# A hybrid decoder trunk on one core: the order of tasks in a step, two more chunks turned on VectorE, one unit more ahead of their high parts, and narrower score matmuls

## Chip, cores and metric

One core of one Trainium2 chip. The metric is the device time of one execution in microseconds (us). Engines are named PE (TensorE, matmuls), DVE (VectorE), ACT (ScalarE), POOL (GpSimd) and SP (which only issues DMAs here).

## What is computed

A decoder of two layers over x, 256 positions x 2048 columns, float32, with 256 memory tokens. Per layer:

```
h = rmsnorm(x); P = h @ W_in        four mixers on columns of P:
  A  forgetting attention, 4 heads x 128 ("fox")
  B  latent attention, low-rank q and kv with a rotary key, 4 heads ("mla")
  C  causal spatial gating unit, 4 groups x 128
  D  differential attention, 4 heads
x += concat(A, B, C, D) @ W_o
x += cross_attention(rmsnorm(x), rmsnorm(mem))      4 heads, W_cq, W_ck, W_cv, W_co
x += (silu(n @ W_gate) * (n @ W_up)) @ W_down, n = rmsnorm(x)     hidden width 5632
```

After the second layer the output is rmsnorm(x).

## The kernel before

**Products in three matmuls.** Each float32 factor is split into a high part (rounded to the fp32r type) and a low part (the rest). A product is hi*hi + hi*lo + lo*hi, each an fp32r matmul. For a weight, ACT casts the high part (`high`, L204) and DVE subtracts it for the low part (`low`, L210). A few units named in `POOLED` (L40) have their low part made on POOL instead.

**Units.** The weight matrices are walked in groups (one output block of 512 columns, or less, over all of its contraction). A group is cut into units of 1024 weight columns: at 512 output columns a unit has two contraction tiles k of 128 rows. `drive` (L227) makes one list of all units of both layers, in order. For each unit it issues the high and low parts of the unit three places ahead (`convert`, `AHEAD = 3`), then the unit's matmuls (at 512 columns: two k, two halves of the positions, three products, 12 matmuls), then the group's `done` if it was the last one, and then `self.step()`. With `hold=1`, used for the first chunk of w_co, the list reads: chunk 0's first unit, chunk 1's first unit, chunk 0's second, chunk 1's second, and then chunks 2 and 3. A chunk of w_co has two units, a chunk of w_o eight.

**Tasks.** Everything between the matmuls is written as Python generators that issue some instructions and then yield. `soon` puts one in the list `urgent`, `later` in the queue `background` (with one empty step ahead of it); only attention heads go there. `step` (L193) advances each urgent task to its next yield, then the first two of the background. A task may wait for others with `wait`, which yields until they are done. Each engine runs its instructions in the order in which they were issued; the kernel's own order is kept (`manual_schedule`). So a step's place in that order says behind what an instruction queues.

**Chunks of x.** x lives as four chunks of 512 columns. When an output block of w_o, w_co or w_down is complete, `into_x` (L945) adds it to its chunk (two DVE adds, L950) and starts a task `norm_chunk` (L342): ACT sums the squares, two yields follow, and then the chunk is turned (positions to the free dimension), and split into high and low parts with the norm's gains (`split_turned`: ACT L206, DVE L212) in two halves, with a yield behind each. There are two ways to turn. Without `early`, `turn` (L414) issues four PE transposes of 128x128 into PSUM for each half. With `early`, `turn_blocks` (L422) issues 16 DVE transposes of 32 partitions x 256 elements (32x32 blocks), four to a step. Before the change, `early` is set for chunks 0 to 2 of w_o in both layers and of the last w_down blocks in the first layer, and never for w_co.

**Who needs a chunk.** A group's operands are a `Split`. Ahead of its matmuls, a unit calls `need(k)` (L104), which drains the tasks of chunk k // 4: it runs them to their end there and then, so that whatever they had not issued comes in front of the unit's matmuls. Behind w_co comes gate: its first unit (k 0 and 1) needs chunk 0, its third chunk 1.

**Heads.** `attend` (L486) takes the MLA and fox heads through scores (L440), mask, exponent, `normalise` (L473, behind a DVE reciprocal L468), transposes and output (L500) over some seven steps. `attend_memory` (L1056) does the same for cross-attention; its first two heads wait for `tq` and `tk` and then take one more empty step (`if h < 2`). `out_v` (L1103) drains two heads and issues their output matmuls (L1116), which read a copy (L1079) of the transposed probabilities. `gate_norm` (L760) and `gate_mix` (L780) are urgent tasks of the gating unit. Fox scores add an fp32r product (rows and own sums of log-forget) to the fp32 product of q and k; the second half of the queries needs 256 keys and the first only 128, but the fp32r product was given 256 columns in both (L439).

Of the kernel before, what the change touches and what calls it, by code (L numbers as in the profile page):

```python
# [12 lines left out]
F32R = mybir.dt.float32r  # L13
# [6 lines left out]
P = 128  # L20
T = 2
S = T * P
# [39 lines left out]
class Task:  # L62
# [5 lines left out]
    def step(self):  # L68
        if not self.done:
            try:  # L70
                next(self.gen)
            except StopIteration:
                self.done = True
# [68 lines left out]
class Kernel:  # L142
# [48 lines left out]
            yield  # L191

    def step(self):  # L193
        for t in list(self.urgent):
            t.step()
        self.urgent = [t for t in self.urgent if not t.done]
        for t in list(self.background)[:2]:
            t.step()
        self.background = deque(t for t in self.background if not t.done)


    def high(self, src, hi, scale=None):
# [24 lines left out]
    def drive(self, groups):  # L227

        units, held = [], []
        for g in groups:  # L230
            i, own = 0, []
            for src, kper in g.blocks:
                b = Block(src, kper * g.ncols)
                step = 1 if not units and not own else 1024 // g.ncols if g.ncols in (256, 512) else 2
                for k0 in range(0, kper, step):
                    n = min(step, kper - k0)
                    own.append(Unit(g, b, k0, n, i))
                    i += n
            if g.hold:
                units, held = units + own[: g.hold], own[g.hold :]  # L240
            else:
                units, held = units + own[: len(held)] + held + own[len(held) :], []
# [99 lines left out]
    def norm_chunk(self, st, c, g, name, early):  # L342

        nc, xs, stats, xc = self.nc, st[0], st[1], self.x[c]
        part = xs.parts[c] = self.split_tile(name)
        for t in range(T):
            self.square_sum(xc[:, t, :], stats[:, t, c : c + 1])
        st[4] += 1
        yield
        yield  # L350
        if early:
            raw = self.slot("xT")
            yield from self.turn_blocks(xc[:], raw)
        for b in range(2):
            tv = raw[:, 2 * b : 2 * b + 2, :] if early else self.turn(xc, 2 * b, 2, "xT")
            self.split_turned(tv, part, 2 * b, self.gains[:, g, 4 * c + 2 * b : 4 * c + 2 * b + 2])
            yield
# [75 lines left out]
    def scores(self, pairs, name="s"):  # L433

        ps = self.bank(name)
        first = True
        for q, off, nk in ((1, 0, S), (0, S, P)):
            for n, (x, y) in enumerate(pairs):
                w = S if x.dtype == F32R else nk  # L439
                self.nc.tensor.matmul(ps[:, off : off + w], x[:, q * P : (q + 1) * P], y[:, :w], start=first, stop=(q == 0 and n == len(pairs) - 1))  # L440
                first = False
        return ps

# [637 lines left out]
    def cross(self, l, norm, st, memT, mres):  # L1081
        s = {}
        y, cT = Split(1), norm[0]

        def out_q(ps):
            nat = self.slot("cq", shape=(P, T, 512))
            self.out_natural(ps, 0, 512, nat, self.times(norm[2][0], 128.0 ** -0.5))
            s["q"] = self.slot("cqT")
            yield
            yield from self.turn_blocks(nat[:], s["q"])  # L1090

        def done_q(ps):
            norm[3].drain()
            s["tq"] = self.soon(out_q(ps))

        def done_k(ps):
            self.mem_rms.drain()
            kT = self.slot("ckT")
            s["tk"] = self.soon(self.out_turned(ps, kT, mres[1]))
            s["p"] = [self.slot("cpT", shape=(P, 2, 512)) for _ in range(2)]  # L1100
            s["heads"] = [self.later(self.attend_memory((s["tq"], s["tk"]), s["q"], kT, h, s["p"][h // 2][:, h % 2, :])) for h in range(4)]

        def out_v(ps, hh):  # L1103
            if hh == 0:
                s["v"] = self.slot("cv", shape=(P, T, 512))
                y.parts[0] = self.split_tile("yc")
            v = s["v"]
            self.out_natural(ps, 0, 256, v[:, :, 256 * hh : 256 * hh + 256], mres[0])
            yield
            for t in s["heads"][2 * hh : 2 * hh + 2]:  # L1110
                t.drain()
            o = self.bank("co")
            for i in range(2):
                h = 2 * hh + i
                for kt in range(2):
                    self.nc.tensor.matmul(o[:, i * S : (i + 1) * S], v[:, kt, h * P : (h + 1) * P], s["p"][hh][:, i, kt * S : (kt + 1) * S], start=(i == 0 and kt == 0), stop=(i == 1 and kt == 1))  # L1116
            ov = o[:].rearrange("p (i s) -> p i s", i=2)
            self.split(ov, y.parts[0][0][:, 2 * hh : 2 * hh + 2, :], y.parts[0][1][:, 2 * hh : 2 * hh + 2, :])

        def done_v(hh):  # L1120
            def f(ps):
                s["tv%d" % hh] = self.soon(out_v(ps, hh))
                if hh == 1:
                    y.tasks[0] = [s["tv0"]]
                    y.late = s["tv1"]
            return f

        yield Group("cq", self.blocks("w_cq", l), 512, cT, False, done_q)
        yield Group("ck", self.blocks("w_ck", l), 512, memT, True, done_k)
        for hh in range(2):  # L1130
            yield Group("cv", self.blocks("w_cv", l, hh, 8), 256, memT, False, done_v(hh))
        for c in range(NC):
            yield Group("wco", self.blocks("w_co", l, c), 512, y, False, self.into_x(c, st, 2 + 3 * l, "fT"), hold=0 if c else 1)


    def ffn(self, l, norm, st):
# [211 lines left out]
```

## Time and profile before

| | |
|---|---|
| median of 3 runs | 2347.46 us (2346.2 to 2347.61) |
| the profiled execution, its own time | 2347.7 us |
| its span in the trace | 2346.0 us, 28353 instructions |
| PE / DVE / ACT / POOL busy | 99% / 64% / 48% / 11% of the span |
| granted PE clock, mean of the span | 0.999 |
| DMA | 444 MB, 189 GB/s |

The span runs from the first to the last instruction on the core; 1.7 us lie outside of it. A busy share is an average over all stages. A matmul's recorded duration is longer than the distance to the next one, since they are pipelined; what one costs is read from the distance of starts. In a timeline a row begins with the start (us from the span's start) and the duration, then engine, line, operation, out<-in, shapes and count; brackets give idle time before it and what ended it.

### The profile page before, as it was taken

What the parts mean: (1) busy time and instruction counts of PE and PEld (TensorE: products, weight loads), DVE (VectorE), ACT (ScalarE), POOL (GpSimd) and SP (SyncE); (2) the same over time, 40 slices, a digit from 0 to 9 for tenths busy, and PEclk for the clock granted to TensorE, in tenths of its full rate; (3) what the DMA queues carried; (4) which work ended last, traced back from release to release, by engine and by line L of the source; (5) the groups of instructions that cost most, each with busy time, mean ns of one, the idle gap of its engine ahead of it and who ended that gap; (6) DMA issues with size and microseconds to landing.
All of it is one profiled execution on the core that took longest, in us unless ns stands there. A gap on an engine that the chain in (4) does not pass through costs nothing.

```text
span 2346.0 us, 28353 instructions
## 1 busy us (share of the span) xinstructions
PE 2324.7 (99%) x10992; PEld 1950.3 (83%) x10992; DVE 1508.6 (64%) x2175; ACT 1132.2 (48%) x1611; POOL 251.3 (11%) x182
## 2 busy tenths in 40 slices
PE   9999999999999999999999999999999999999998
PEld 8888878888888888888898888798888888888886
DVE  6856687655766446767766666866666664476564
ACT  7656555644443334444455555545444443434443
POOL 1222341100000000000012314411000000000000
PEclk9999999999999999999999999999999999999999
DMA  8654555455455555555545454554555555555643
GB/s 293 223 177 154 186 189 188 164 193 200 179 208 195 189 197 181 196 200 184 203 164 193 161 176 159 201 197 162 197 180 197 202 194 196 197 180 192 221 179 126
DMA packets 69719, 444.24 MB, mean 189 GB/s; under 512 B 8000, under 2 KB 10064, under 8 KB 19920
## 3 DMA queue, kind: packets, MB, share of 16 engines
q1 hardware_dynamic: 67328, 435.52, 52.4%
q0 software_dynamic: 2112, 6.85, 0.9%
q8 instruction: 86, 1.41, 0.2%
q14 instruction: 49, 0.40, 0.0%
q10 hardware_dynamic: 144, 0.06, 0.0%
HBM read 440.30 MB, written 2.10 MB: 189 GB/s over the span
## 4 chain that ended last, share of the span: by engine, by line
PE 88%; DVE 4%; ACT 2%; DMA 2%; issue 1%; POOL 1%; SPq 0%; POOLq 0%; ACTq 0%; DVEq 0%
PE gate L305 7%; PE gate L304 7%; PE gate L303 7%; PE up L305 7%; PE up L304 7%; PE up L303 7%; PE down L303 7%; PE down L305 7%; PE down L304 7%; DVE wlo L210 1%; PE wo L305 1%; PE wo L303 1%; PE wo L304 1%; ACT whi L204 1%; DVE xT L428 1%
## 5 line engine op out<-in xcount | busy, mean ns | idle before, releaser
L210 DVE TENSOR_TENSOR wlo<-raw,whi 128x1024 fp32r<-128x1024 f32 (+3 forms) x764 | 933.5, 1235 | 572.4 <-ACT whi L204 566.2
L204 ACT CAST whi<-raw 128x1024 fp32r<-128x1024 f32 (+2 forms) x828 | 842.3, 1037 | 633.8 <-PE up L305 246.6
L303 PE MATMUL gate<-whi,fT_hi 128*128 128x512 f32 x704 | 274.7, 390 | 0.0
L305 PE MATMUL gate<-whi,fT_lo 128*128 128x512 f32 x704 | 274.0, 389 | 0.0
L304 PE MATMUL gate<-wlo,fT_hi 128*128 128x512 f32 x704 | 273.9, 389 | 0.0
L303 PE MATMUL up<-whi,fT_hi 128*128 128x512 f32 x704 | 273.9, 389 | 0.0
L304 PE MATMUL up<-wlo,fT_hi 128*128 128x512 f32 x704 | 273.9, 389 | 0.0
L305 PE MATMUL up<-whi,fT_lo 128*128 128x512 f32 x704 | 273.9, 389 | 0.0
L303 PE MATMUL down<-whi,hid_hi 128*128 128x512 f32 x704 | 273.9, 389 | 0.0
L304 PE MATMUL down<-wlo,hid_hi 128*128 128x512 f32 x704 | 273.9, 389 | 0.0
L305 PE MATMUL down<-whi,hid_lo 128*128 128x512 f32 x704 | 273.9, 389 | 0.0
L210 POOL TENSOR_TENSOR wlo<-raw,whi 128x1024 fp32r<-128x1024 f32 x64 | 165.3, 2587 | 408.4 <-ACT whi L204 408.2
L428 DVE STREAM_TRANSPOSE hidT<-silu 32x256 f32<-32x256 f32 x352 | 153.3, 436 | 5.7
L305 PEld LDWEIGHTS down<-whi,hid_lo 128*128 128x128 f32 x704 | 132.2, 188 | 27.6
L305 PEld LDWEIGHTS gate<-whi,fT_lo 128*128 128x128 f32 x704 | 132.2, 188 | 27.5
L304 PEld LDWEIGHTS up<-wlo,fT_hi 128*128 128x128 f32 x704 | 132.2, 188 | 27.5
L303 PEld LDWEIGHTS up<-whi,fT_hi 128*128 128x128 f32 x704 | 132.2, 188 | 27.5
L305 PEld LDWEIGHTS up<-whi,fT_lo 128*128 128x128 f32 x704 | 132.2, 188 | 27.3
L304 PEld LDWEIGHTS down<-wlo,hid_hi 128*128 128x128 f32 x704 | 132.2, 188 | 27.3
L303 PEld LDWEIGHTS down<-whi,hid_hi 128*128 128x128 f32 x704 | 132.2, 188 | 27.3
L304 PEld LDWEIGHTS gate<-wlo,fT_hi 128*128 128x128 f32 x704 | 132.2, 188 | 27.2
L303 PEld LDWEIGHTS gate<-whi,fT_hi 128*128 128x128 f32 x704 | 132.2, 188 | 27.2
(426 smaller groups left out, 3347.1 us busy)
## 6 DMA issues: line engine op xcount, KB each, us to landing
raw<-in_w_gate SPq DMA_DIRECT2D x88, 1024.0 KB, 4.8
raw<-in_w_up SPq DMA_DIRECT2D x88, 1024.0 KB, 4.7
raw<-in_w_down SPq DMA_DIRECT2D x88, 1024.0 KB, 4.8
raw<-in_w_o SPq DMA_DIRECT2D x32, 1024.0 KB, 4.8
raw<-in_w_dk SPq DMA_DIRECT2D x8, 1024.0 KB, 5.1
raw<-in_w_dv SPq DMA_DIRECT2D x8, 1024.0 KB, 6.5
raw<-in_w_fq SPq DMA_DIRECT2D x8, 1024.0 KB, 4.9
raw<-in_w_fk SPq DMA_DIRECT2D x8, 1024.0 KB, 4.8
```

The lines of the kernel that those rows point to most:

```text
L204: self.nc.scalar.copy(hi, src)
L210: (eng or self.nc.vector).tensor_tensor(out=lo, in0=src, in1=hi.bitcast(F32), op=ALU.subtract)
L303: mm(o, xh, wh, start=(i == 0), stop=False)
L304: mm(o, xh, wl, start=False, stop=False)
L305: mm(o, xl, wh, start=False, stop=(i == len(g.ks) - 1))
L428: self.nc.vector.transpose(o[:, :, :, a, :], src[32 * a : 32 * a + 32, :, :, b, :])
```

## The change

Four edits. `step` advances the first two background tasks (the heads) ahead of the urgent ones. `norm_chunk` yields once more between an early chunk's DVE transposes and its high parts, so these come one unit later. `scores` gives the fp32r product the same number of columns as the fp32 product, 128 for the first half of the queries. `into_x` of w_co gets `early` for chunks 0 and 1, in both layers.

```diff
--- before.py
+++ after.py
@@ -191,12 +191,12 @@
             yield
 
     def step(self):
+        for t in list(self.background)[:2]:
+            t.step()
+        self.background = deque(t for t in self.background if not t.done)
         for t in list(self.urgent):
             t.step()
         self.urgent = [t for t in self.urgent if not t.done]
-        for t in list(self.background)[:2]:
-            t.step()
-        self.background = deque(t for t in self.background if not t.done)
 
 
     def high(self, src, hi, scale=None):
@@ -351,6 +351,7 @@
         if early:
             raw = self.slot("xT")
             yield from self.turn_blocks(xc[:], raw)
+            yield
         for b in range(2):
             tv = raw[:, 2 * b : 2 * b + 2, :] if early else self.turn(xc, 2 * b, 2, "xT")
             self.split_turned(tv, part, 2 * b, self.gains[:, g, 4 * c + 2 * b : 4 * c + 2 * b + 2])
@@ -436,8 +437,7 @@
         first = True
         for q, off, nk in ((1, 0, S), (0, S, P)):
             for n, (x, y) in enumerate(pairs):
-                w = S if x.dtype == F32R else nk
-                self.nc.tensor.matmul(ps[:, off : off + w], x[:, q * P : (q + 1) * P], y[:, :w], start=first, stop=(q == 0 and n == len(pairs) - 1))
+                self.nc.tensor.matmul(ps[:, off : off + nk], x[:, q * P : (q + 1) * P], y[:, :nk], start=first, stop=(q == 0 and n == len(pairs) - 1))
                 first = False
         return ps
 
@@ -1130,7 +1130,7 @@
         for hh in range(2):
             yield Group("cv", self.blocks("w_cv", l, hh, 8), 256, memT, False, done_v(hh))
         for c in range(NC):
-            yield Group("wco", self.blocks("w_co", l, c), 512, y, False, self.into_x(c, st, 2 + 3 * l, "fT"), hold=0 if c else 1)
+            yield Group("wco", self.blocks("w_co", l, c), 512, y, False, self.into_x(c, st, 2 + 3 * l, "fT", c < 2), hold=0 if c else 1)
 
 
     def ffn(self, l, norm, st):
```

## Rows read from the trace of the kernel before

**Rows 1.** The page, part 1: busy time (share of the span), instructions.
```profile
PE 2324.7 (99%) x10992; PEld 1950.3 (83%) x10992; DVE 1508.6 (64%) x2175; ACT 1132.2 (48%) x1611; POOL 251.3 (11%) x182
```

**Rows 2.** TensorE's waits: engine, line, what it waited for; us in total, times, longest.
```profile
PE wo L304 <- DVE wlo L210: 3.5, 4, 1.5
PE fpt L479 <- ACT fp L473: 3.0, 2, 1.5
PE cq L304 <- POOL wlo L210: 1.2, 3, 0.6
PE fo L500 <- ACT fptt L483: 1.1, 2, 0.6
```

**Rows 3.** Busy time in a stretch: PE, PEld, DVE, ACT, POOL; clock; DMA; GB/s.
```profile
438.06:453.73 15.67, 15.67 (x81) 13.00 (x79) 11.15 (x18) 12.04 (x25) 2.41 (x1) 1.00 0.41 141
```

**Rows 4.** Timeline of DVE at w_co's end: start, us, instruction, idle before.
```profile
444.01 1.22 DVE L210 TENSOR_TENSOR wlo<-raw,whi 128x1024 fp32r<-128x1024 f32 x1 [1.95 <-ACT whi L204]
445.16 0.87 DVE L212 SCALAR_TENSOR_TENSOR fT_lo<-xT,gains,fT_hi 128x256 fp32r<-128x256 f32 x2
...
447.08 1.28 DVE L950 TENSOR_TENSOR x<-wco,x 128x512 f32<-128x512 f32 x2
```

**Rows 5.** Timeline of TensorE, the same stretch and gate's first units.
```profile
443.07 0.39 PE L305 MATMUL wco<-whi,yc_lo 128*128 128x512 f32 x1
443.31 0.60 PE L419 MATMUL xT<-ident,x 128*128 128x128 f32 x4
...
443.98 0.40 PE L304 MATMUL wco<-wlo,yc_hi 128*128 128x512 f32 x1
...
454.27 0.40 PE L305 MATMUL gate<-whi,fT_lo 128*128 128x512 f32 x1
...
460.68 0.40 PE L305 MATMUL gate<-whi,fT_lo 128*128 128x512 f32 x1
```

**Rows 6.** Timeline of ACT, the same stretch.
```profile
442.95 1.03 ACT L204 CAST whi<-raw 128x1024 fp32r<-128x1024 f32 x1
...
454.01 0.84 ACT L206 ACTIVATE fT_hi<-xT,gains 128x256 fp32r<-128x256 f32 x2 [1.30 <-PE xT L419]
```

**Rows 7.** Tile xT, DVE's lines: count, ns min/median/max, first and last start.
```profile
L428 DVE STREAM_TRANSPOSE xT<-x x144: 425/436/442, 298.0 to 1513.3; 32x256 f32<-32x256 f32 x144
...
L212 DVE SCALAR_TENSOR_TENSOR fT_lo<-xT,gains,fT_hi x32: 473/478/485, 445.2 to 1628.6; 128x256 fp32r<-128x256 f32 x32
```

**Rows 8.** The end: TensorE's last matmul, and the last stretch (columns of rows 3).
```profile
2336.91 0.39 PE L305 MATMUL down<-whi,hid_lo 128*128 128x512 f32 x1
...
2340.00:2346.00 6.00, 0.00 (x0) 0.00 (x0) 1.45 (x3) 0.63 (x1) 0.00 (x0) 0.57 0.46 175
```

**Rows 9.** Timeline of DVE ahead of the fox wait, layer 0.
```profile
247.33 0.75 DVE L776 SCALAR_TENSOR_TENSOR v<-v,mv,lnw 128x512 f32<-128x512 f32 x1
248.11 0.75 DVE L777 SCALAR_TENSOR_TENSOR v<-v,lnr,lnw 128x512 f32<-128x512 f32 x1
...
249.44 0.16 DVE L468 RECIPROCAL inv<-sums 128x2 f32<-128x2 f32 x1
```

**Rows 10.** Timeline of TensorE, the drained fox head.
```profile
281.85 0.70 PE L500 MATMUL fo<-fptt,fv 128*128 128x256 f32 x2 [0.57 <-ACT fptt L483]
```

**Rows 11.** Timeline of DVE in the w_o stage, layer 0.
```profile
315.23 5.16 DVE L212 SCALAR_TENSOR_TENSOR cT_lo<-xT,gains,cT_hi 128x256 fp32r<-128x256 f32 x2
...
324.02 1.22 DVE L210 TENSOR_TENSOR wlo<-raw,whi 128x1024 fp32r<-128x1024 f32 x1
```

**Rows 12.** Timeline of TensorE: fp32 with 128 columns, fp32r with 256.
```profile
209.08 0.39 PE L530 MATMUL do<-dv,dptt 128*128 128x128 f32 x2
209.31 0.39 PE L531 MATMUL do<-dv,dptt 128*128 128x128 f32 x2
...
375.32 0.28 PE L315 MATMUL ck<-memTs_hi,whi 128*128 128x256 f32 x1
375.44 0.28 PE L316 MATMUL ck<-memTs_lo,whi 128*128 128x256 f32 x1
```

## Prediction

> **What bounds the kernel now.** Read first: the page's busy shares. TensorE is busy 99% of the span, DVE 64% [rows 1]; only two things can shorten this kernel, less TensorE work or fewer of its few gaps, and anything that makes TensorE wait lengthens it one for one. Second: TensorE's waits. The largest sum to 3.5 us for low parts of w_o's weights, 3.0 for fox probabilities, 1.2 and 1.1 [rows 2], so little is to be won. Third: the stretch that the change loads, from w_co's first finished chunk to the first gate matmul. TensorE is busy in all of its 15.67 us, but DVE is busy 11.15 us of it already [rows 3]. So a mean of 64% hides a stretch with 4.5 us of DVE time free. Fourth: that stretch instruction by instruction on DVE, TensorE and ACT [rows 4 to 6]; DVE's order there is the program's order.
>
> **The change, part by part.** I sum against the profiled execution: span 2346.0, its own time 2347.7, the median of the runs 2347.46, so differences carry over to the median as they are.
>
> *1. Two chunks turned on DVE.* Removed: two chunks in two layers, eight TensorE transposes each, 32 in all. Between 443.07 and 443.98 two matmul steps of 0.227 and four transposes pass [rows 5]: 0.91 - 0.455 = 0.455, or 0.114 us each, so 32 are worth 3.6 us.
> By the Trainium skill (TensorE: Matmul & The Clock Gate, Part 4) a transpose of this kind takes some 275 ns in a kernel; by that the saving would be 8.8 us. The trace's durations are like it, but the starts are 0.114 apart, and the starts decide.
>
> Added: 16 DVE transposes of 0.436 us per chunk [rows 7], four to a step, 1.78 a step (4 x 0.436 and the small gaps between). Where do they go? The units run in the order w0a, w1a, w0b, w1b, w2a, w2b, w3a, w3b, g0, g1, g2 (hold=1; two units a chunk of w_co, then gate). Chunk 0 is done after w0b, so its task steps there: squares; w1b: nothing; w2a, w2b, w3a, w3b: four transposes each; then the new empty step; then two steps of high and low parts. But g0 reads chunk 0, and its need(0) drains the task: all that is left is issued on the spot, right ahead of g0's matmuls. Chunk 1 is one unit later; its last four transposes come after g0, and g2 drains it. In the w_o stage the same task has eight units a chunk; here it has two.
>
> Everything on DVE ahead of chunk 0's first low part is therefore queued in this order, from the w3b weights' low part, which starts at 444.01 after its high part [rows 4, 6] and has nothing new ahead of it: five wlo (w3b, g0, g1, g2, g3) x 1.23 = 6.15; two x adds (chunks 2 and 3) x 1.28 = 2.56; seven steps of transposes (four of chunk 0, three of chunk 1) x 1.78 = 12.46; chunk 2's low pair 0.87 and the first low of chunk 0, 0.48 [rows 4, 7] = 1.35. Sum 22.5. None of these waits on something later than itself (chunk 3's sum is ready at about 451.5, ACT's parts take 0.84 [rows 6]). So the third matmul of gate, the first that reads a low part, can start at 444.0 + 22.5 = 466.5, against 454.27 [rows 5]: 12.2 us late. Cost of the second wait: g0 and g1 follow at full speed and would bring g2's third matmul to about 466.5 + 10 x 0.227 + 0.455 + 12 x 0.227 + 0.455 + 2 x 0.227 = 472.9. DVE until then: rest of chunk 0's lows 1.3 (467.8), chunk 1's last step 1.78 (469.6), chunk 2's second low pair, which waits for its transposes after g0 (471.0), wlo of g4 (472.4), chunk 3's low pair after g1 (474.1), two small statistics and wlo of g5 (475.9), chunk 1's first low (476.4). g2's third matmul thus starts at 476.4, against 460.68 [rows 5]: **15.7 us a layer**. The saved transposes are inside this comparison, since both ends are starts on TensorE; with DVE as the bound they buy nothing here. After g2 the stages have no new DVE work (chunks 2 and 3 are turned as before), so nothing is given back either.
>
> The clock: TensorE would stand idle from about 452 (454.27 less two steps of 0.227 and the sixteen saved transposes of 0.114) to 462.7 (chunk 0's last transposes end after 18.2 of the 22.5 us, at 462.2, and its first high part takes 0.5). The trace shows one such standstill: the last matmul starts at 2336.91, and the last six microseconds have a granted clock of 0.57, that is mostly the lower level, 1.2 GHz [rows 8]. Here the standstill is longer than that tail. At 1.2 GHz a matmul takes twice as long. If all of g0 and g1 ran so, g2's third matmul would come 5.6 us later still (chunk 2's and 3's transposes on TensorE are late, ACT's high parts behind them, DVE's queue behind those): 21.3 a layer. No row shows how soon the clock comes back, so the bounds are 15.7 and 21.3; I take 18, the middle, since g0's start is surely slow and g1's not surely.
> The Trainium skill (TensorE: Matmul & The Clock Gate, Part 1) says that an idle array falls to half its clock and has to be busy again before it gets it back; by that 15.7 is too low. The tail row agrees on the fall; no row shows the return.
>
> Two layers: 36 us, bounds 24.4 (only the first wait counts, no clock) and 42.6.
>
> *2. Heads first in a step.* Order inside a step changes, and a head that waits for an urgent task now sees it done one unit later. (a) Fox: TensorE waits 1.5 us in each layer for a reciprocal that DVE reaches at 249.44 behind two gate_norm operations of 0.75 [rows 2, 9]. Heads first puts it ahead of its step's pair: of 1.5 us some 1.3 go, 2.6 for both layers; bounds 0 and 3.0. (b) Cross-attention: the first two heads wait for tk, which ends in the very step in which they look; they start one unit later, so their transposes fall into the step in which out_v drains them, and co follows cpt with only the copy between. The nearest row is the drained fox head, 0.57 us [rows 10]; twice a layer, four times: +2.2, bounds 0 and 3. The MLA heads also start one unit later (rotation), and the differential and fox heads after them; w_o's order leaves them room, the last fox head is drained at w_o as now. Cost 0.
>
> *3. The empty step* in w_o and w_down: chunk highs come one unit later; with eight or more units a chunk and four or more left before the next reader, nothing waits. What it may move is a collision: two low parts of 0.48 take 5.16 us at 315.23, the wlo behind starts at 324.02 [rows 11], and that is the 3.5 us of w_o's wait. Taken 0; bounds -3.5 (gone) and +3.2 (one more pair of such lows, about 2 x 1.6).
>
> *4. Narrow fox scores:* 8 matmuls have 128 columns instead of 256. A 256-column fp32r matmul takes 0.12 and a 128-column fp32 one 0.226 [rows 12]. If narrow fp32r is as a transpose, 8 x 0.006 is saved; if as fp32, 8 x 0.1 is lost: -0.1 to +0.9. Taken 0, by the starts 0.114 of a 128-column transpose.
>
> Sum: +36 - 2.6 + 2.2 = **+35.6 us, 2383 us**.
>
> **The rivals.** *Only the first wait* (chance 0.10): DVE reaches chunk 1 in time because ACT's and TensorE's parts come earlier than I put them, and the clock costs nothing: +24.4 - 0.4, 2371.5. For it: 12.2 comes from rows alone. Against: chunk 1's drain has four transposes and four other DVE operations ahead of it. *The clock stays low* (0.10) through g0 and g1: +42.6 - 0.4, 2389.7. *No wait at gate, faster* (0.04): DVE's queue would have to bring chunk 0's first low by 454.3, that is 22.5 us of work in 10.3. It decides at that point alone: if the tasks were stepped so that chunk 1's transposes and the late wlo come behind chunk 0, some 10 to 12 us less, the wait would vanish. Then -3.6 - 2.6 + 2.2 = -4.0, 2343.5; if cross-attention loses nothing either, 2341.3. Against it: DVE's order in the trace is the program's. *No change* (0.02): waits of about 2 us a layer just eat the savings, 2347.5.
>
> **How the numbers follow.** Forecast, both waits and some clock: 0.74, 2383. Range: from 24.4 with w_o's wait gone (24.4 - 2.6 + 1 - 3.5 = 19.3, 2367) to 42.6 with the collisions (42.6 - 0.4 + 3.2 + 2, 2395). A measurement of this kernel can tell about 0.2% (4.7 us) from no change. Slower by more: 0.74 + 0.10 + 0.10 = 0.94; faster by more, half of that rival, since 2343.5 and 2341.3 lie on both sides of the bound: 0.02; within: 0.02 + 0.02 = 0.04.
>
> **What would show it.** Right: gate's third matmul waits for DVE's fT_lo some 12 us in each layer, its unit g2 some 3 to 6, granted clock under 1 just there; 64 xT transposes more on DVE and 32 fewer on TensorE (88 to 56); the wait for fox's probabilities near 0.3; new waits of co for cpT of about 0.5. The forecast is wrong if gate's first unit starts within 2 us of w_co's end, or if ACT or the weights' high parts, not DVE's queue, end the wait.

## The result, and the profile of the changed kernel

The changed kernel takes 2381.39 us (median of 4 runs, 2380.22 to 2381.88) against 2347.09 in the runs of the kernel before beside it: a ratio of 1.0146, 95% interval 1.0128 to 1.0163. It is 34.3 us slower; 35.6 was forecast. The kernel before ran again beside each group of experiments, with medians of 2346.74 to 2347.08.

The page of the changed kernel, its first lines, to be read beside [rows 1]:

```profile
span 2380.0 us, 28333 instructions
PE 2330.0 (98%) x10960; PEld 1952.7 (82%) x10960; DVE 1530.8 (64%) x2239; ACT 1132.6 (48%) x1611; POOL 249.3 (10%) x182
```

TensorE has 32 instructions fewer and DVE 64 more. The busy shares hardly move (DVE is at 64% in both), so the page alone would not tell where 34 us went. The waits do. TensorE's waits (engine, line, what it waited for; us in total, times, longest), beside [rows 2]:

```profile
PE gate L303 <- ACT fT_hi L206: 25.9, 4, 10.7
PE gate L305 <- DVE fT_lo L212: 6.0, 4, 2.5
PE fo L500 <- DVE u L789: 2.4, 2, 1.2
...
PE co L1116 <- ACT cpT L1079: 1.0, 4, 0.2
```

Two lines at gate make 31.9 us, where the kernel before had no entry. Three entries of [rows 2] are gone: w_o's low parts (3.5), the fox probabilities (3.0) and the drained fox head (1.1). Two small ones are new: fo behind u, and co behind cpT.

TensorE's timeline at gate's first units in layer 0, beside [rows 5]:

```profile
460.79 0.79 PE L303 MATMUL gate<-whi,fT_hi 128*128 128x512 f32 x1 [10.67 <-ACT fT_hi L206]
...
464.48 0.80 PE L305 MATMUL gate<-whi,fT_lo 128*128 128x512 f32 x1 [2.48 <-DVE fT_lo L212]
465.08 0.63 PE L303 MATMUL gate<-whi,fT_hi 128*128 128x512 f32 x1
465.50 0.63 PE L304 MATMUL gate<-wlo,fT_hi 128*128 128x512 f32 x1
...
468.49 0.58 PE L305 MATMUL gate<-whi,fT_lo 128*128 128x512 f32 x1
...
469.57 0.39 PE L304 MATMUL gate<-wlo,fT_hi 128*128 128x512 f32 x1
469.80 0.40 PE L305 MATMUL gate<-whi,fT_lo 128*128 128x512 f32 x1
...
474.96 0.50 PE L303 MATMUL gate<-whi,fT_hi 128*128 128x512 f32 x1 [2.27 <-ACT fT_hi L206]
...
476.21 0.80 PE L305 MATMUL gate<-whi,fT_lo 128*128 128x512 f32 x1 [0.52 <-DVE fT_lo L212]
476.80 0.63 PE L303 MATMUL gate<-whi,fT_hi 128*128 128x512 f32 x1
```

The first unit of gate waits 10.67 us for the first high part of chunk 0 and again 2.48 for its first low part. Then its matmuls start 0.43 apart, down to the last at 468.49; the second unit's are 0.23 apart. The third unit (chunk 1) waits once more, 2.27 and 0.52. Its next matmul starts 0.59 later and the following ones 0.43 apart, down to the one at 478.94; from 479.25 on the distance is 0.23 again. The granted clock by stretch (columns as in [rows 3]) says the same of the first unit:

```profile
450.00:460.00 10.00, 0.11 (x2) 0.00 (x0) 9.71 (x19) 3.13 (x8) 0.00 (x0) 0.76 0.30 105
460.00:465.00 5.00, 1.74 (x3) 1.00 (x4) 4.91 (x11) 1.93 (x5) 0.00 (x0) 0.50 0.00 0
```

DVE is busy for 9.71 of the ten microseconds in which TensorE stands still, and a clock of 0.50 is the lower level, 1.2 GHz. DVE's timeline, beside [rows 4]:

```profile
436.11 1.29 DVE L950 TENSOR_TENSOR x<-wco,x 128x512 f32<-128x512 f32 x2 [0.39 <-PE wco L305]
...
442.07 1.23 DVE L210 TENSOR_TENSOR wlo<-raw,whi 128x1024 fp32r<-128x1024 f32 x1 [1.95 <-ACT whi L204]
...
458.40 3.62 DVE L429 STREAM_TRANSPOSE xT<-x 32x256 f32<-32x256 f32 x8
...
463.95 1.67 DVE L212 SCALAR_TENSOR_TENSOR fT_lo<-xT,gains,fT_hi 128x256 fp32r<-128x256 f32 x4
...
475.68 1.67 DVE L212 SCALAR_TENSOR_TENSOR fT_lo<-xT,gains,fT_hi 128x256 fp32r<-128x256 f32 x4
```

The add of chunk 0 comes 1.95 us earlier than before (436.11 against the 438.06 at which [rows 3] begin), so earlier stages gained; but from the w3b weights' low part at 442.07 to chunk 0's first low part at 463.95 DVE works without waiting for anything. The first wait is listed under ACT, whose high part ended it. That high part reads chunk 0's last transposes, the first four of the row at 458.40 (to about 460.2). ACT itself comes free in the same moment:

```profile
457.86 0.63 ACT L336 ACTIVATE junk<-x 128x512 f32<-128x512 f32 x1 [6.83 <-DVE x L950]
...
460.23 1.71 ACT L206 ACTIVATE fT_hi<-xT,gains 128x256 fp32r<-128x256 f32 x4
```

Between the two rows ACT has chunk 3's squares and one high part of weights to do, and it could begin them only when DVE had made that chunk's add, for which it had waited 6.83 us. Both ways lead back to DVE's queue. The low parts at 463.95 and 475.68 release the third matmul of the first and of the third unit, at 464.48 and 476.21.

How much each stretch lost is best read from starts, by the first start of w_co and of up (the number behind the three durations). Before:

```profile
L303 PE MATMUL wco<-whi,yc_hi x64: 389/391/580, 427.9 to 1616.4; 128*128 128x512 f32 x64
L303 PE MATMUL up<-whi,fT_hi x704: 389/389/389, 477.1 to 2227.7; 128*128 128x512 f32 x176
```

After:

```profile
L303 PE MATMUL wco<-whi,yc_hi x64: 389/389/580, 424.6 to 1628.9; 128*128 128x512 f32 x64
L303 PE MATMUL up<-whi,fT_hi x704: 389/389/389, 494.0 to 2261.6; 128*128 128x512 f32 x176
```

From w_co's first matmul to up's first it is 49.2 us before and, by the timelines' second decimal, 69.5 after: **20.3 more in layer 0**. In layer 1 the same starts are 1591.60 and 1640.81 before, 1604.65 and 1674.80 after: 20.9 more. The lower clock lasts a little longer there (the four transposes behind gate's first unit take 0.71 us to the next start, 0.36 in layer 0). Ahead of w_co the changed kernel gains: 3.3 us in layer 0 (427.9 to 424.6) and 3.9 from up's first start in layer 0 to w_co's in layer 1. 20.3 + 20.9 - 3.3 - 3.9 is the 34.0 of the spans.

### The profile page after: what moved, and what is told of

Its sections match the earlier page's. It is cut to its first block, busy times and chain, and to the rows that moved or that the text cites. A ratio compares the mean times of both kernels' runs of the same rounds, so it can differ in the third digit from the quotient of the medians.

```text
span 2380.0 us, 28333 instructions
## 1 busy us (share of the span) xinstructions
PE 2330.0 (98%) x10960; PEld 1952.7 (82%) x10960; DVE 1530.8 (64%) x2239; ACT 1132.6 (48%) x1611; POOL 249.3 (10%) x182
## 4 chain that ended last, share of the span: by engine, by line
PE 84%; issue 5%; DVE 4%; POOL 3%; ACT 2%; DMA 2%; SPq 0%; POOLq 0%; DVEq 0%; ACTq 0%
PE gate L305 7%; PE gate L303 7%; PE gate L304 7%; PE up L305 7%; PE up L304 7%; PE up L303 7%; PE down L303 7%; PE down L304 7%; PE down L305 7%; DVE wlo L210 1%; POOL wlo L210 1%; DVE xT L429 1%; ACT whi L204 1%; PE wo L303 1%; PE wo L305 1%
```

## The experiments

**Which part costs.** First the change without the turn on DVE in w_co, the turn alone on top of the kernel before, and the change with chunk 0 alone turned on DVE.

The first, against the kernel after:

```diff
--- after.py
+++ a1_no_wco_turn.py
-            yield Group("wco", self.blocks("w_co", l, c), 512, y, False, self.into_x(c, st, 2 + 3 * l, "fT", c < 2), hold=0 if c else 1)
+            yield Group("wco", self.blocks("w_co", l, c), 512, y, False, self.into_x(c, st, 2 + 3 * l, "fT"), hold=0 if c else 1)
```

> The changed kernel with w_co's chunks turned on TensorE as before; the other three edits stay. Theory (the two chunks turned on DVE carry the whole loss, the rest of the change gains): in the changed kernel the first add of w_co's chunk 0 starts 1.95 us earlier than before, and everything behind it loses 18.9 a layer, so this kernel takes 2381.4 - 2 x 18.9 = 2343.6 us, 3.5 less than before, and no wait stands at gate. Rival (the new order of the step is part of the wait at gate, since tasks are issued later): some of the wait stays, 2350 to 2370 us.

Measured: 2343.08 us, ratio 0.9983 (0.9974 to 0.9991). No wait is left at gate. All of the loss hangs on the w_co turn; the other three edits together gain a little.

The second has the same two lines the other way round, against the kernel before:

```diff
--- before.py
+++ a2_wco_turn_only.py
-            yield Group("wco", self.blocks("w_co", l, c), 512, y, False, self.into_x(c, st, 2 + 3 * l, "fT"), hold=0 if c else 1)
+            yield Group("wco", self.blocks("w_co", l, c), 512, y, False, self.into_x(c, st, 2 + 3 * l, "fT", c < 2), hold=0 if c else 1)
```

> The kernel before with nothing but the two chunks of w_co turned on DVE (no empty step, old order of the step, wide scores). Theory (the loss is DVE's queue ahead of gate and adds up with the rest): 2347.1 + 2 x 18.9 = 2384.9 us, first wait at gate 13 us a layer (ACT and DVE parts together), second about 3. Rival (the empty step is what makes chunk 0 late): without it the task ends a step sooner, the drain finds less to do, and the wait at gate shrinks by a unit of 2.7 us a layer, 2379 us or less.

Measured: 2376.03 us, ratio 1.0120 (1.0106 to 1.0134), 28.9 more than before. The time is the rival's: alone, the turn costs 38.3 - 28.9 = 9.4 us less than it adds to the other three edits (2381.39 against 2343.08). Its mechanism is not borne out, for it had the wait for chunk 0 shrink. TensorE's waits at gate in this kernel:

```profile
PE gate L303 <- ACT fT_hi L206: 21.4, 2, 10.7
PE gate L305 <- DVE fT_lo L212: 4.9, 2, 2.5
```

The first wait is as long as in the whole change (10.7, then 2.5), but there are two of each, not four: the third unit does not wait here.

The third, against the kernel after:

```diff
--- after.py
+++ a3_chunk0_only.py
-            yield Group("wco", self.blocks("w_co", l, c), 512, y, False, self.into_x(c, st, 2 + 3 * l, "fT", c < 2), hold=0 if c else 1)
+            yield Group("wco", self.blocks("w_co", l, c), 512, y, False, self.into_x(c, st, 2 + 3 * l, "fT", c < 1), hold=0 if c else 1)
```

> The changed kernel with chunk 0 alone turned on DVE, chunk 1 on TensorE. Theory (volume of DVE's queue): ahead of chunk 0's first low part three steps of transposes fall out (5.3 us) and chunk 1's four low parts come in (1.7), so the first wait shortens by 3.7 us; the second wait (2.8) and its slow clock (2) go; 0.9 of TensorE transposes come back: about 8 us a layer less, 2365 us. Rival (what counts is that chunk 0 is drained at gate, whatever stands in between): the first wait stays as it is at 13 us, only the second goes, 4 to 5 us a layer less, 2372 us.

Measured: 2364.18 us, ratio 1.0069 (1.0056 to 1.0083), 21.1 above the kernel without the turn, against 38.3 for two chunks. One chunk on DVE costs somewhat over half of two: it goes by DVE's volume ahead of gate, as the theory said (the place of the work counts too, as b3 below shows). Chunk 1's transposes stand in DVE's queue ahead of chunk 0's parts, and without them the first wait is 7.7 instead of 10.7:

```profile
PE gate L303 <- ACT fT_hi L206: 15.3, 2, 7.7
```

**The other edits alone**, on top of the kernel before. The step order:

```diff
--- before.py
+++ b1_heads_only.py
+        for t in list(self.background)[:2]:
+            t.step()
+        self.background = deque(t for t in self.background if not t.done)
         for t in list(self.urgent):
             t.step()
         self.urgent = [t for t in self.urgent if not t.done]
-        for t in list(self.background)[:2]:
-            t.step()
-        self.background = deque(t for t in self.background if not t.done)
```

> The kernel before with nothing but the new order of the step. Theory (gains and losses of it are small and nearly cancel): of the waits of before, fox probabilities (3.0) and the drained fox head (1.1) go, and a wait of the fox head's output for the bank that the gating unit's DVE work holds (2.4) and of co for cpT (1.0) come: 0.7 us less, 2346.4, within noise of before. Rival (the order also ends w_o's wait of 3.5 us for low parts, since heads that start a unit later shift DVE's queue there): 2343.

Measured: 2348.37 us, ratio 1.0006 (0.9997 to 1.0015): nothing that can be told from no change. Its waits show why:

```profile
PE wo L304 <- DVE wlo L210: 3.5, 4, 1.4
PE fo L500 <- DVE u L789: 2.4, 2, 1.2
```

The fox wait (3.0) and the drained head's (1.1) are gone, and two others have come in their place, fo's and that of co for cpT (1.0, as in the change); w_o's stays.

The empty step:

```diff
--- before.py
+++ b2_empty_step_only.py
             yield from self.turn_blocks(xc[:], raw)
+            yield
```

> The kernel before with nothing but the empty step ahead of the high parts. Theory (it is the empty step that ends w_o's wait: low parts no longer stand in DVE's queue while POOL works): that wait of 3.5 us is gone, 2343.6 us, the other waits stay. Rival (the order of the step ended it): the wait stays, 2347.1 us.

Measured: 2340.81 us, ratio 0.9976 (0.9968 to 0.9985), faster than both kernels and by more than expected (6.2 us, not 3.5). w_o's wait is gone, so it was the empty step that ended it, not the order of the heads. DVE's timeline there:

```profile
313.48 3.02 DVE L212 SCALAR_TENSOR_TENSOR cT_lo<-xT,gains,cT_hi 128x256 fp32r<-128x256 f32 x2
...
321.28 1.23 DVE L210 TENSOR_TENSOR wlo<-raw,whi 128x1024 fp32r<-128x1024 f32 x1
```

and POOL's:

```profile
312.46 3.36 POOL L210 TENSOR_TENSOR wlo<-raw,whi 128x1024 fp32r<-128x1024 f32 x1 [1.53 <-ACT whi L204]
```

Before, the two low parts of [rows 11] took 5.16 us from 315.23, beside two low parts of weights on POOL:

```profile
314.61 5.49 POOL L210 TENSOR_TENSOR wlo<-raw,whi 128x1024 fp32r<-128x1024 f32 x2 [3.28 <-ACT whi L204]
```

One unit later, the two pairs fall differently against POOL's work: the pair takes 3.02, and the weights' low part behind it comes at 321.28 instead of 324.02. That the overlap with POOL stretches DVE's operation is read from these rows; no run moved POOL's work alone.

**Why the whole is worse than its parts.** The turn alone (+28.9), the empty step alone (-6.2) and the heads alone (+1.4) add up to 24.1; the change costs 34.3. Ten microseconds are left. The suspect is the empty step inside w_co: with it all of chunk 1's parts are left to the third unit's drain, without it the first half goes out behind the second unit:

```diff
--- after.py
+++ c3_no_empty_wco.py
-            yield
+            if early != 2:
+                yield
...
-            yield Group("wco", self.blocks("w_co", l, c), 512, y, False, self.into_x(c, st, 2 + 3 * l, "fT", c < 2), hold=0 if c else 1)
+            yield Group("wco", self.blocks("w_co", l, c), 512, y, False, self.into_x(c, st, 2 + 3 * l, "fT", 2 if c < 2 else False), hold=0 if c else 1)
```

> After with the empty step left out for the two w_co chunks alone (it stays in the other turned stages). Theory: the second wait at the feed-forward's second unit and its slow clock come from that step, as they are missing where the w_co turn runs without it; that is about 4.4 us a layer, 2 x 4.4 = 8.8 less than 2381.4, so 2372.6. Rival: the empty step in w_co costs nothing and the sum over the single parts misses the whole for another reason, 2380 to 2382.

Measured: 2371.22 us, ratio 1.0106 (1.0092 to 1.0120), 10.2 below the change (1.4 more than expected). Its waits and its starts:

```profile
PE gate L303 <- ACT fT_hi L206: 21.3, 2, 10.7
PE gate L305 <- DVE fT_lo L212: 5.0, 2, 2.5
```

```profile
L303 PE MATMUL wco<-whi,yc_hi x64: 389/389/579, 423.2 to 1622.8; 128*128 128x512 f32 x64
...
L303 PE MATMUL up<-whi,fT_hi x704: 389/389/389, 487.8 to 2250.9; 128*128 128x512 f32 x176
```

The second wait of each layer is gone, and from w_co to up it takes 64.6 us instead of 69.5, 4.9 less, and in layer 1 4.6 less (1598.54 to 1664.08): 9.5 of the 10.2. So the empty step is good in w_o and bad in w_co: there the next reader is one unit away.

**The clock.** Two kernels fill TensorE's standstill with matmuls whose result nobody reads, so that only the clock should differ.

In the first, 40 of them stand ahead of gate's first unit:

```diff
--- after.py
+++ a4_fill.py
+        def fill():
+            idle = self.tbank("fill")
+            for i in range(40):
+                nc.tensor.matmul(idle[:, :P], self.ones[:], self.ones[:], start=(i == 0), stop=(i == 39))
...
-                yield Group("gate", self.blocks("w_gate", l, j), 512, fT, False, done_gate)
+                yield Group("gate", self.blocks("w_gate", l, j), 512, fT, False, done_gate, begin=fill if j == 0 else None)
```

> The changed kernel with 40 extra fp32 matmuls of 128 columns (two passes of 0.113 each, about 9 us in all) on TensorE ahead of the first gate unit of each layer, in the time in which it stood idle; their result is not read. Theory (the clock's fall costs time on top of DVE's queue): the granted clock stays at 1 through the wait, the matmuls of gate's first unit start 0.227 apart instead of 0.427, g0 ends 2 us sooner, and what hangs on it (chunk 2's transposes, ACT, DVE, chunk 1) too; 2 to 3.5 us a layer less, 2374 to 2377 us. Rival (DVE's queue alone sets when gate's third unit can start, the clock is hidden): within 1 us of 2381.4.

Measured: 2381.74 us, ratio 1.0144 (1.0128 to 1.0159). It does not decide: the first matmuls now ran at the full level, but the clock fell in the next wait, for the low part.

```profile
461.82 0.40 PE L304 MATMUL gate<-wlo,fT_hi 128*128 128x512 f32 x1
465.18 0.80 PE L305 MATMUL gate<-whi,fT_lo 128*128 128x512 f32 x1 [2.96 <-DVE fT_lo L212]
465.77 0.63 PE L303 MATMUL gate<-whi,fT_hi 128*128 128x512 f32 x1
```

In the second, 46 stand there and 13 more ahead of the third matmul:

```diff
--- a4_fill.py
+++ b4_fill_both.py
+                if g.begin is not None and g.name == "gate" and i == 0 and t == 0:
+                    g.begin(13)
...
-        def fill():
+        def fill(n=46):
             idle = self.tbank("fill")
-            for i in range(40):
-                nc.tensor.matmul(idle[:, :P], self.ones[:], self.ones[:], start=(i == 0), stop=(i == 39))
+            for i in range(n):
+                nc.tensor.matmul(idle[:, :P], self.ones[:], self.ones[:], start=(i == 0), stop=(i == n - 1))
```

> As the fill of before, but with fill matmuls in both gaps of gate's first unit: 46 (10.4 us) ahead of it and 13 (2.9 us) between its second and third matmul, where TensorE waits for the low part and where the clock fell in the first fill. Their result is not read. Theory (the slow clock costs time behind the wait): granted clock 1 up to gate's third unit, g0's matmuls 0.227 apart, 2 to 4 us a layer less than the changed kernel, 2373 to 2377 us. Rival (hidden behind DVE's queue): 2380 to 2382 us.

Measured: 2380.17 us, ratio 1.0140 (1.0127 to 1.0153). All of the first unit now runs at the full level (starts 0.23 apart), but the second fill itself waited 1.53 us for low parts on DVE before it began, and then ran for 2.9 us, past the 463.8 at which chunk 0's first low part was ready:

```profile
462.39 3.14 PE L1145 MATMUL fill<-ones 128*128 128x128 f32 x26 [1.53 <-DVE fT_lo L212]
465.29 0.47 PE L307 MATMUL gate<-whi,fT_lo 128*128 128x512 f32 x1
```

So this run gives the clock back and takes about as much away, and the price of the clock has to be read from the rows of the change itself: nine distances take 4.01 us in the first unit (464.48 to 468.49) where nine of 0.227 are 2.04, so 2.0 us, and in the third unit some 1.4 by the same count (seven distances, 476.21 to 479.25, take 3.04 instead of 1.59). No run isolates it.

**Place or volume?** In b3 w_co's chunks are turned earlier: eight transposes to a step, without the empty steps.

```diff
--- after.py
+++ b3_early_steps.py
-        yield
+        if early != 8:
+            yield
...
-            yield from self.turn_blocks(xc[:], raw)
-            yield
+            yield from self.turn_blocks(xc[:], raw, 8 if early == 8 else 4)
+            if early != 8:
+                yield
...
-            yield Group("wco", self.blocks("w_co", l, c), 512, y, False, self.into_x(c, st, 2 + 3 * l, "fT", c < 2), hold=0 if c else 1)
+            yield Group("wco", self.blocks("w_co", l, c), 512, y, False, self.into_x(c, st, 2 + 3 * l, "fT", 8 if c < 2 else False), hold=0 if c else 1)
```

> The changed kernel in which a chunk of w_co that is turned on DVE takes its transposes eight to a step and has neither the second empty step behind the squares nor the new one behind the transposes: the same instructions, issued earlier, so that chunk 0 is complete ahead of gate's first unit and nothing is left to drain. Theory (both count: DVE's queue is too long by itself, and the late place of the parts in it adds to it): chunk 0's first low part ends near 457.3, gate's third unit loses some 5 to 6 us a layer against before instead of 19, 2352 to 2358 us. Rival (volume alone, 28 us of transposes in a stretch that is full): 2375 us or more. Second rival (place alone): no wait left, 2343 us.

Measured: 2360.63 us, ratio 1.0057 (1.0044 to 1.0070). Some 21 of 38 us come back by place alone, so both count. The range was missed by 3 us; the waits that took gate's place lie with the chunks still turned on TensorE:

```profile
PE xT L422 <- DVE x L952: 8.9, 3, 4.3
PE xT L422 <- DVE fT_lo L212: 5.3, 2, 2.6
```

With chunks 0 and 1 ahead in DVE's queue, the adds of chunks 2 and 3 come late, and their transposes on TensorE wait for them. Gate's first unit again runs at the lower level behind that wait (starts 0.43 apart from 455.03 to 457.59). So with the place mended the volume still costs some 17.5 us (2360.63 against the 2343.08 without the turn), on other instructions.

**A version that beats both.** Without the w_co turn, two candidates: the change less the turn and less the empty step that the first two cross-attention heads take; and the kernel before with the empty step and the narrow scores.

```diff
--- after.py
+++ c1_best.py
-        if h < 2:
-            yield
...
-            yield Group("wco", self.blocks("w_co", l, c), 512, y, False, self.into_x(c, st, 2 + 3 * l, "fT", c < 2), hold=0 if c else 1)
+            yield Group("wco", self.blocks("w_co", l, c), 512, y, False, self.into_x(c, st, 2 + 3 * l, "fT"), hold=0 if c else 1)
```

> After without the w_co turn on DVE (2343.1 when run alone) and without the empty unit that attend_memory yields for heads 0 and 1 ahead of its scores, so that with the heads first their co comes one step earlier or later than its cpT. Theory: the waits of co for cpT (4 x 0.24 = 1.0 in that run) go and nothing comes in their place, some 2342. Rival: the step only moves the wait to another pair of operations (score to exponential), 2343 to 2345.

Measured: **2339.79 us**, ratio 0.9971 (0.9960 to 0.9981), the lowest median of all, 2 us under the expectation and not to be told apart from the empty step alone. In its waits co no longer stands; the longest left is fo's, 2.4.

The second candidate:

```diff
--- before.py
+++ c2_empty_narrow.py
             yield from self.turn_blocks(xc[:], raw)
+            yield
...
-                w = S if x.dtype == F32R else nk
-                self.nc.tensor.matmul(ps[:, off : off + w], x[:, q * P : (q + 1) * P], y[:, :w], start=first, stop=(q == 0 and n == len(pairs) - 1))
+                self.nc.tensor.matmul(ps[:, off : off + nk], x[:, q * P : (q + 1) * P], y[:, :nk], start=first, stop=(q == 0 and n == len(pairs) - 1))
```

> Before with the empty step between DVE's transposes and their high parts (2340.8 alone) and the narrow scores of the fox heads (128 columns in place of 256 for the second part), without the other two parts of the change. Theory: 8 fox heads save about 0.06 us each, 2340.3. Rival: narrow fp32r matmuls cost as much as or more than wide ones, 2340.8 to 2342.

Measured: 2341.31 us, ratio 0.9976 (0.9967 to 0.9985), as with the empty step alone. The narrow scores give and cost nothing that these runs can tell. The head's four score operations end at the same distance: after,

```profile
264.76 0.28 PE L440 MATMUL fs<-rows,own 128*128 128x256 f32 x1
...
265.56 0.48 PE L303 MATMUL wo<-whi,yd_hi 128*128 128x512 f32 x1
```

and before,

```profile
261.61 0.28 PE L440 MATMUL fs<-rows,own 128*128 128x256 f32 x1
...
262.41 0.48 PE L303 MATMUL wo<-whi,yd_hi 128*128 128x512 f32 x1
```

0.80 us from the first of them to the next unit, in both.

## Why the prediction was right, point by point

**What bounds.** Right: the stretch from w_co's first chunk to gate, with little DVE time free [rows 3], was where the change was paid for, and the mean of 64% hid it.

**Part 1, the queue of 22.5 us.** Right almost to the digit. The queue was summed from the w3b low part's start to the end of chunk 0's first low part; that is 442.07 to 464.4 (463.95 and its 0.48), 22.4 us, and the third matmul starts at 464.48. Gate's first matmul was put at 462.7 and starts at 460.79 + 1.95 = 462.74. Against [rows 5], and with the 1.95 us by which the stage now begins earlier, the third is 464.48 + 1.95 - 454.27 = 12.2 us late, the number forecast. The third unit's third matmul was put at 476.4 without any slow clock; it starts at 476.21 + 1.95 = 478.2, 17.5 us later than [rows 5]. The sign of being wrong, that ACT ends the wait, is there in the list's name alone: ACT had itself been waiting for DVE, as its rows above show, and with fewer transposes in DVE's queue (a3) the wait is 7.7 instead of 10.7.

What the 32 removed transposes are worth, 3.6 us by their starts or, as an estimate, 8.8 by the figure of the Trainium skill (TensorE: Matmul & The Clock Gate, Part 4; it stands there beside one for bf16, the blocks here are float32), no run shows: where they are missing DVE sets the time.

**The clock.** Right in kind: the lower level is there where it was looked for, in all of the first unit and, which had been left open, not in the second. 18 was taken as the middle of the bounds 15.7 and 21.3 (the middle is 18.5); with the slow matmuls behind the third unit's wait, 1.4 us, the rows give 17.5 + 1.4 = 18.9. From w_co to up it is 20.3 and 20.9 in the two layers, of which 1.3 each come with the heads (Part 2b): 18.9 and 19.6. The term of 36 was 38.5. That an idle array falls to half its clock and has to be busy again first, which the Trainium skill says (TensorE: Matmul & The Clock Gate, Part 1), is what the trace shows here, at 1.2 GHz over the first unit after 10.67 us of waiting.

**Part 1, what was not seen.** The prediction listed the empty step in the order of chunk 0's steps and priced it nowhere. By c3 it carries 10.2 of the 38 us: the whole second wait is its doing. The sum of part 1 was right because the queue was written out instruction by instruction with the step in it; a forecast that had added up the edits' prices one by one would have come out 10 us low, at the 24 of the single kernels.

**Part 2a, fox.** In the list the wait of 3.0 is gone altogether. By starts some of it is left:

```profile
249.03 0.39 PE L305 MATMUL u<-whi,hT_lo 128*128 128x512 f32 x1
249.53 0.33 PE L479 MATMUL fpt<-ident,fp 128*128 128x128 f32 x1
```

0.50 where 0.23 is the rule, so 0.27 a layer remains, the 0.3 that was forecast. The drained head's wait, which the prediction took to stay as it was, went too. But a head that runs earlier meets another wait, which no part of the prediction has: fo's bank is held by the gating unit's product until DVE has read it into u. TensorE's timeline:

```profile
256.98 0.39 PE L305 MATMUL wo<-whi,ym_lo 128*128 128x512 f32 x1
258.56 0.67 PE L500 MATMUL fo<-fptt,fv 128*128 128x256 f32 x2 [1.20 <-DVE u L789]
```

From start to start 1.58 where 0.23 is the rule, 1.35 lost in each layer. Per layer the fox heads save 1.39 (248.66 to 250.55 before, 1.66 over the rule, less the 0.27) and 0.74 (281.00 to 281.85, less 0.11) and lose 1.35: 0.8, or 1.6 us in both layers, not 2.6.

**Part 2b, cross-attention.** +2.2 was taken, from 0.57 a time. The list of waits says 0.24 a time, but the starts bear the 0.57 out:

```profile
427.32 1.04 PE L1078 MATMUL cpt<-ident,cp 128*128 128x128 f32 x8
428.60 1.99 PE L1116 MATMUL co<-cpT,cv 128*128 128x256 f32 x8 [0.24 <-ACT cpT L1079]
430.24 0.58 PE L303 MATMUL wco<-whi,yc_hi 128*128 128x512 f32 x1
```

The transposes take 1.28 to the next start and co 1.64, where the kernel before had 0.79 (427.06 to 427.85) and 1.54 (430.68 to 432.22): 0.59 lost, four times 2.4. In c1, which removes it, w_co to up is back from 50.5 us (in a1) to the 49.2 of the kernel before. Of these 1.3 only 0.6 is a loss: the second pair's transposes, 0.79, stood ahead of w_co's first matmul before and now stand behind it. The first pair loses its 0.6 ahead of w_co.

**Part 3, the empty step outside w_co.** Mis-sized: 0 was taken, with a lower bound of -3.5. Alone the step saves 6.2 us. In the change about 5.2 of it is left: of the 7.2 us that the kernel is shorter ahead of w_co (3.3 and 3.9), 1.6 are the transposes that moved behind its first matmul and 1.6 the fox heads, while the first cross-attention pair loses 1.2 there. Both are beyond the bound. What the bound missed is that the idle time before a matmul, on which [rows 2] rest, counts from a modelled end 0.39 behind the start, while the next start is due after 0.23. So 0.16 us of each wait goes unlisted: the 1.46 at 325.30 before is 1.85 from start to start, 1.62 lost, and of 352.95 to 353.44, 0.49 where 0.23 is the rule, nothing is listed. By starts w_o's four waits cost 4.1 us, not 3.5, and those of cq behind them, which the bound left out, 2.6, of which 1.4 stays in b2. That makes 5.3 of the 6.2; the rest is not traced.

**Part 4.** Right: nothing.

**The rivals.** Only the first wait: the case needed chunk 1 in time, and it was not (it is in c3, without the empty step in w_co, at 2371.2 where the rival stood at 2371.5, but by chance: the rival had no cost of the clock, which c3 pays, and no gain from the empty step, which c3 has). Clock low through the second unit: no, starts 0.23 apart from 469.57 on. No wait at gate: b3 shows that the order of the tasks does decide, but that DVE's volume then delays chunks 2 and 3. The terms as measured: 38.5 - 1.6 + 2.4 - 5.2 = 34.1, where the spans differ by 34.0, for 36 - 2.6 + 2.2 + 0 = 35.6. So the mechanism of part 1 was right, and that the total came so near is in part luck: part 1 was 2.5 too low, and the empty step, taken at nothing, 5.2 too high.

## What to carry to other kernels

Before moving work to an engine with time to spare, look at its busy time in the stretch between the work's producer and its first reader, and write its queue down in program order: a mean of 64% was no help, the queue gave 12.2 us to the digit. Every empty step between producer and consumer should be judged at each place it is used: the same yield was worth 6 us where eight units follow and cost 10 where one does. And price single edits together, since here they added up to 24 us alone and to 34 in one kernel.

## What the runs showed of the hardware

- The idle time listed before a matmul is 0.16 us less than what a wait costs from start to start (1.20 listed, 1.35 lost at fo; 0.24 listed, 0.59 lost at co with its slower neighbours). Many small waits can hide in this.
- A wait of 2.96 us for a low part was followed by matmuls at the lower clock level (starts 0.43 apart) although 9.1 us of fill had run ahead of it (a4); between fill and wait there were another wait, 1.73, and two matmuls at the full level.
- Two low parts of a chunk on DVE took 5.16, 3.02 or 0.87 us, the long ones beside a low part of weights on POOL.
